# A two-layer encoder trunk on one core: later scores, scaled copies in the bias tiles, grouped head norms, two more warming products, token halves apart in the last unit

## The chip, the cores and the metric

The kernel runs on one core of a Trainium2 chip. The metric is device microseconds of one execution, as a median over several runs. Before the change it is 2175.67 us, the median of 3 runs that lie between 2174.48 and 2177.18 us. One further execution was taken by the hardware profiler; all rows below come from it.

## The reference, cut to what matters

256 tokens of width 2048 pass through two layers. Both have 16 heads of 128 and a squared-ReLU MLP of width 8192. Everything is float32.

```python
# layer 1
u = rms_norm(h, a_norm_g)
q, k, v, fz = split(u @ a_w_in)                 # 2048 -> 3*2048 + 16
q, k = rms_norm(q per head), rms_norm(k per head)
logf = log_sigmoid(fz + a_b_f)                  # c = cumsum over tokens
s = q @ k.T * scale + c[query] - c[key]         # causal
h = h + softmax(s) @ v @ a_w_out
h = h + sq(relu(rms_norm(h) @ w1)) @ w2
# shared keys and values
k, v = split(rms_norm(h) @ kv_w);  k = rms_norm(k per head)
# layer 2
q = rms_norm(rms_norm(h) @ b_w_q per head)
s = q @ k.T * scale + bias[clipped distance]    # by chunks of 64
h = h + softmax(s) @ v @ b_w_out
h = h + sq(relu(rms_norm(h) @ w1)) @ w2
```

## The kernel before, in words

**Weights and units.** Every weight matrix comes in *units* of 128 x 1024 float32 (512 KB): two slices of 128 rows of the inner dimension, for the same 512 output columns. A unit is loaded by SyncE (`load`, L128, tile `raw`, 4 buffers), split by ScalarE into a rounded part `hi` (L144) and by VectorE into the remainder `lo` (L145; `issue`, L137, 3 buffers each), and used by TensorE in 12 products of 512 columns (`products`, L318): for each of the 2 slices and each of the 2 blocks `b` of 128 tokens, activations-hi by weights-hi (L324), hi by lo (L325) and lo by hi (L326). `fetch` (L148) splits two units ahead of the one that is used and keeps three loads ahead of that. A *panel* (`panels`, L328) is 8 units: the whole inner dimension of 2048 for 512 output columns of both token blocks. Its sums stand in one of two PSUM tiles `acc` of two banks, one bank for each token block. After the last unit the panel's `evac` is called for block 0 and then for block 1. A *woven* stage runs its first two panels in turn, unit by unit.

**Order.** `keep_order` (L36) pins VectorE, ScalarE, TensorE and SyncE to the order in which the Python text issues their instructions. So each of the four is a queue in written order, and an instruction that waits holds back all that stand behind it on its engine. GpSimd has few instructions.

**The fill queue.** All work beside the products is put into `fill`, a list of lists. After the 12 products of each unit `run_fill` (L157) takes the next list and issues what is in it. `add_fill` (L457) lays a sequence of lists over the head of the queue, one list for each coming unit. So "item 7" of an added sequence is issued after the products of the eighth unit from then on. A unit takes about 2.7 us.

**Turning.** TensorE needs the inner dimension on the partitions. VectorE transposes blocks of 32 x 32 into a tile `z` (L210, 2 buffers); `carry` (L213) writes `z` to a DRAM tile `turn` with one transfer and, two units later (one for the small softmax tiles), reads it back with four transfers (L226), which SyncE can issue only when the first has landed.

**Layer 1 attention.** For each group of 4 heads there is a q panel, a k panel and a v panel. `head_norm` (L347) squares the sums on ScalarE (L356), adds them by head on VectorE (L358), forms the root on GpSimd (L364), and in later units scales and turns them (L368, L210). `attend` (L434) is added after the k panel: it makes the bias tile (items 2, 5, 6), and for head `a` of the group runs `softmax` in four steps from item 7 + 3a: the score products on TensorE (L396, L397), bias and maximum on VectorE, exponentials on ScalarE, division and transposition on VectorE. The turned probabilities `prT` come back over DRAM, and `values` (L425) uses them 8 items after the scores. In the last group of a layer the heads follow each other by 2 items.

**Between the layers.** `next_x` (L234) forms each new residual block, turns it, and `split_turned` (L185) scales it by the norm gains into a tile `y` of the `z` buffers (L190) and splits that into hi (L193) and lo (L194). At the end of layer 1 this is done twice, for layer 2's queries (`xb`) and, in reversed token order, for the shared keys and values (`xkv`, L626, items 13 to 20 of the query stage). The query stage has four panels, the first two woven. For its first group `head_norm` copies the sums out of PSUM first (`copied`, L354), so that the third panel can have the `acc` tile.

**Start and end.** Before the first weights are there, 9 products of ones run on TensorE (L89). At the end, L391 adds the last panel's sums to the residual for one token block after the other, and L673 stores each.

Of the kernel before, what the change touches and what calls it, by code (L numbers as in the profile page):

```python
# [9 lines left out]
F32 = mybir.dt.float32  # L10
F32R = mybir.dt.float32r
AF = mybir.ActivationFunctionType
ALU = mybir.AluOpType
AX = mybir.AxisListType

P = 128
T = 256
NB = T // P
D = 2048
KT = D // P  # L20
H = 16
GH = 4
NG = H // GH
# [6 lines left out]
EARLY = 3  # L30
UA = UN // 512
REL = 384
GAP = 3


def keep_order(tc, engines):  # L36
# [11 lines left out]
def trunk(ctx: ExitStack, tc: tile.TileContext, xT, xr, gs, hg, bf, wgate, w_in, w_oa, w1a, w2a,  # L48
          w_kv, w_qb, w_ob, w1b, w2b, rel, out):
    nc = tc.nc  # L50
    V, S, G, TE, SY = nc.vector, nc.scalar, nc.gpsimd, nc.tensor, nc.sync
# [8 lines left out]
    qkv = pool("qkv", 2)  # L60
# [24 lines left out]
    ones = const.tile([P, T], F32, name="ones")  # L85
    V.memset(ones, 1.0)
    warm = ps_o.tile([P, 512], F32, name="pt", tag="po")
    for _ in range(9):
        TE.matmul(warm[:, :P], ones[:, :P], ones[:, :P], start=True, stop=True)  # L89
    mhalf = const.tile([P, GH], F32, name="mhalf")  # L90
    V.memset(mhalf, -0.5)
# [92 lines left out]

    def split_turned(t, n, which, into):  # L185
        x = acts.tile([P, 2, GH, T], F32R, name="act")
        y = qkv.tile([P, GH * T], F32, name="z").rearrange("p (k t) -> p k t", k=GH)
        for j in range(GH):
            m = which * KT + GH * n + j
            S.activation(y[:, j].rearrange("p (b i c) -> p b i c", b=NB, i=4), t[:, j], AF.Copy, scale=gsb[:, m : m + 1])  # L190
            if j == 1:
                yield
        S.activation(x[:, 0], y, AF.Copy)  # L193
        V.tensor_tensor(x[:, 1], y, x[:, 0].bitcast(F32), op=ALU.subtract)  # L194
        into.extend(x[:, :, j, :] for j in range(GH))
        yield
# [16 lines left out]
    def carry(z, dst, wait=1):  # L213
        w = z.shape[1]
        n = w // 4
        box = []

        def rows():
            box.append(dram.tile([P, w], F32, name="turn", tag=f"turn{w}", bufs=4))
            SY.dma_start(box[0], z)  # L220

        def columns():
            s = box[0].rearrange("(i a) f -> a i f", i=4)
            d = dst.rearrange("p (i f) -> p i f", i=4)
            for j in range(4):
                SY.dma_start(d[32 * j : 32 * j + 32], s[:, :, j * n : (j + 1) * n])  # L226

        return [[rows]] + [[]] * wait + [[columns], [], []]
# [86 lines left out]
            f.r, f.e = root(f.ms, f.name), scaled(f.ms, f.name)  # L315
            self.flipped = f

    def products(ps, hi, lo, x, u):  # L318
        for j in range(UA):
            k = u * UA + j  # L320
            wh, wl = hi[:, j * 512 : (j + 1) * 512], lo[:, j * 512 : (j + 1) * 512]
            for b in range(NB):
                xh, xl = (x[k][:, i, b * P : (b + 1) * P] for i in range(2))
                TE.matmul(ps[b], xh, wh, start=k == 0, stop=False)  # L324
                TE.matmul(ps[b], xh, wl, start=False, stop=False)  # L325
                TE.matmul(ps[b], xl, wh, start=False, stop=k == KT - 1)  # L326

    def panels(x, evacs, before=None):  # L328
        ps = [acc_pair() for _ in evacs]
        for u in range(KT // UA):  # L330
            if before:
                before(u)
            for q, evac in enumerate(evacs):
                hi, lo = fetch(min(u // 2, AHEAD), 2) if before else fetch()
                products(ps[q], hi, lo, x, u)
                run_fill()
                if u == KT // UA - 1:
                    for b in range(NB):
                        evac(b, ps[q][b])
# [7 lines left out]
    def head_norm(stats, z, dst, late=0, copied=False):  # L347
        rest = []

        def f(b, ps):  # L350
            src = ps
            if copied:
                src = wk.tile([P, 512], F32, name="qc", tag="wk")
                V.tensor_copy(src, ps)  # L354
            sq = wk.tile([P, 512], F32, name="sq", tag="wk")
            S.activation(sq, ps, AF.Square)  # L356
            ss = sm.tile([P, GH], F32, name="ss")
            V.tensor_reduce(ss, sq.rearrange("p (a d) -> p a d", a=GH), axis=AX.X, op=ALU.add)  # L358
            rn = sm.tile([P, GH], F32, name="rn")

            def norm():
                vv = sm.tile([P, GH], F32, name="vv")
                V.tensor_scalar(vv, ss, 1.0 / P, stats().e[:, b : b + 1], op0=ALU.mult, op1=ALU.add)  # L363
                G.tensor_tensor(rn, vv, mhalf, op=ALU.pow)  # L364

            def turn():
                qn = wk.tile([P, 512], F32, name="qn", tag="wk")
                V.tensor_tensor(qn.rearrange("p (a d) -> p a d", a=GH), src.rearrange("p (a d) -> p a d", a=GH),  # L368
                                rn.unsqueeze(2).to_broadcast([P, GH, P]), op=ALU.mult)
                blocks32(qn, z, b)  # L370

            rest.append((norm, turn))
            if not late:
                norm()
            if b == NB - 1:
                add_fill([[]] * (late - 1) + ([[n for n, _ in rest]] if late else []) + [[t] for _, t in rest] + carry(z, dst))
        return f

    def scale_q(land, layer):
# [45 lines left out]
    def values(st, a, v, o, i):  # L425
        po = ps_o.tile([P, 512], F32, name="po", tag="po")
        pT = st["pT"].rearrange("p (i n c) -> p n i c", i=4, c=32)
        TE.matmul(po[:, :T], v[:, 0, a * P : (a + 1) * P], pT[:, :2], start=True, stop=False)  # L428
        TE.matmul(po[:, P:T], v[:, 1, a * P : (a + 1) * P], pT[:, 2], start=False, stop=True)  # L429
        o[i] = quarter(i)  # L430
        S.activation(o[i][:, 0], po[:, :T], AF.Copy)  # L431
        V.tensor_tensor(o[i][:, 1], po[:, :T], o[i][:, 0].bitcast(F32), op=ALU.subtract)  # L432

    def attend(g, q, k, v, cq, o, make_bias, gap):  # L434
        st = [{} for _ in range(GH)]
        box = {}
        k4 = k.rearrange("p (i a b c) -> p a b i c", i=4, a=GH, b=NB)
        items = [[] for _ in range(15 + gap * GH)]
        step = steps(lambda: make_bias(g, box))
        items[2].append(step)  # L440
        items[5].append(step)
        items[6].append(step)
        for a in range(GH):
            at = 7 + gap * a
            step = steps(lambda a=a: softmax(st[a], g, a, q(), k4, box["b"], cq() if cq else None))
            for i in range(4):
                items[at + i].append(step)
            items[at + 3].append(lambda a=a: add_fill(st[a]["carry"]))
            items[at + 8].append(lambda a=a: values(st[a], a, v, o, g * GH + a))
        return items  # L450

    def v_evac(v, r):
# [4 lines left out]
    def add_fill(items):  # L457
        for i, it in enumerate(items):
            if i < len(fill):
                fill[i] = fill[i] + it  # L460
            else:
                fill.append(it)
# [3 lines left out]
    x = []  # L466
# [33 lines left out]
    def gates(x, st):  # L500
# [44 lines left out]
        def turn_c():  # L545
            pc = ps_o.tile([P, 512], F32, name="pt", tag="po")
            ct["cq"] = const.tile([P, NB, H], F32, name="cq")
            for b in range(NB):
# [2 lines left out]

        step, spread = steps(logs), steps(st.spread)
        return [[clear], [], [parts], [lambda: products(range(8))], [lambda: products(range(8, KT))], [spread], [spread],
                [step], [step], [step], [], [], [turn_c]]

    def decay_bias(g, box):
        nb = qkv.tile([P, GH, REL], F32, name="bias")
# [11 lines left out]
    for g in range(NG):  # L569
        zq, lq = turned("z")  # L570
        qb = {}
        late = 6 if g == 0 else 0
        panels(x, [head_norm(lambda: st0, zq, lq, late)], begin if g == 0 else None)
        if g == 0:
            step = steps(head_gains)
            add_fill([[step], [], [], [], [step]])
            add_fill([[lambda i=i: rows_in(i)] for i in range(5, 8)])
            add_fill([[lambda i=i: st0.add(*chunks[i])] for i in range(3, 8)])
            fill[4].insert(len(fill[4]), st0.roots)
            add_fill(gates(x, st0))  # L580
        add_fill([[]] * (7 + late) + [[lambda qb=qb, lq=lq: qb.update(q=scale_q(lq, 0))]])
        zk, k = turned("k")
        v = qkv.tile([P, NB, 512], F32, name="v")
        panels(x, [head_norm(lambda: st0, zk, k)])
        add_fill(attend(g, lambda qb=qb: qb["q"], k, v, lambda: ct["cq"], o, decay_bias, GAP if g < NG - 1 else 2))
        panels(x, [v_evac(v, st0.r)])

    def mlp(x, st, last):
# [34 lines left out]
    mlp(x1, st1, lambda n, r2: next_x(n, r2, st2, 3, xb, kept))  # L623
    xkv = []
    again = [steps(lambda n=n: kept[n](True, 2, xkv)) for n in range(NG)]
    add_fill([[], [], [st2.both], [], [st2.flip]] + [[]] * 8 + [[again[i // 2]] for i in range(2 * NG)])  # L626


    qs, evs = [], []
# [26 lines left out]
    for g in range(NG):  # L656
        zk, k = turned("k")
        v = qkv.tile([P, NB, 512], F32, name="v")
        panels(xkv, [head_norm(lambda: st2.flipped, zk, k)])
        add_fill(attend(g, lambda g=g: qs[g], k, v, None, o, rel_bias, GAP if g < NG - 1 else 2))  # L660
        panels(xkv, [v_evac(v, st2.flipped.r)])

    st3, x3 = RowStats("n"), []
# [66 lines left out]
```

## Time and profile before

| | us |
|---|---|
| median of 3 runs | 2175.67 |
| the profiled execution | 2172.02 |
| its span in the trace | 2169.8 |
| TensorE busy in the span | 2151.4 (99%) |
| VectorE busy | 1280.5 (59%) |
| ScalarE busy | 1048.8 (48%) |

The page of the profile gives, for the whole span, busy time by engine and the costliest groups of instructions. The waits view adds up, for each engine and line, the time that the engine sat idle and what ended it. The timeline gives single instructions with start and duration; a product of 512 columns is shown as busy for 0.39 us, although in full flow the next starts 0.227 us after it, since successive products overlap in the array. So the time lost at a wait is the distance between two starts less 0.227 us, which is 0.16 us more than the idle time shown. The windows view gives the TensorE clock that was granted in a stretch, as a share of full speed.

### The profile page before, as it was taken

To read this page: it belongs to the slowest core of one execution; us is meant where nothing else is said; L and a number is where in the kernel's file an instruction comes from. 1 tells how busy PE (TensorE), PEld (TensorE's weight loads), DVE (VectorE), ACT (ScalarE), POOL (GpSimd) and SP (SyncE) were. 2 spreads that over 40 slices of the span, in tenths; PEclk is the share of its full clock that TensorE was granted. 3 is DMA by queue.
4 is the path that set the end of the run, shared out by engine and by line. 5 is a ranking of instruction groups with operands and counts; after the bars stand their busy time and mean duration, and the time that the engine had idled before them with its cause. 6 is when DMAs were issued, how large, how long until landed. Compare 5 with 4: busy or idle time off the path is not lost.

```text
span 2169.8 us, 25773 instructions
## 1 busy us (share of the span) xinstructions
PE 2151.4 (99%) x9514; PEld 1776.5 (82%) x9514; DVE 1280.5 (59%) x1465; ACT 1048.8 (48%) x1251; POOL 48.4 (2%) x47
## 2 busy tenths in 40 slices
PE   9999999999999999999999999999999999999999
PEld 8778888888888888888877888888888888888887
DVE  6767766655555555555667667765554555555554
ACT  6544445554344344345555445455543543443443
POOL 1010000000000000000001001000000000000000
PEclk9999999999999999999999999999999999999999
DMA  7776787786676577677767777777866766766774
GB/s 277 240 237 223 229 253 232 235 265 199 207 238 214 194 244 221 194 232 232 229 211 247 245 227 225 243 239 243 250 195 213 242 203 203 243 213 194 240 225 165
DMA packets 183886, 491.60 MB, mean 227 GB/s; under 512 B 36928, under 2 KB 73936, under 8 KB 183760
## 3 DMA queue, kind: packets, MB, share of 16 engines
q1 hardware_dynamic: 183760, 489.96, 71.7%
q8 instruction: 74, 1.21, 0.2%
q14 instruction: 52, 0.43, 0.1%
HBM read 450.01 MB, written 39.87 MB: 226 GB/s over the span
## 4 chain that ended last, share of the span: by engine, by line
PE 92%; DMA 4%; DVE 2%; ACT 1%; SPq 1%; issue 1%; DVEq 0%; ACTq 0%
PE acc L325 30%; PE acc L324 30%; PE acc L326 30%; DMA k<-turn 1%; DMA turn<-z 1%; DVE lo L145 1%; PE s L397 1%; PE po L428 1%; ACT hi L144 1%; SPq L226 0%; DMA prT<-turn 0%; PE s L396 0%; DMA raw<-in_w2a 0%; DVE qn L368 0%; PE po L429 0%
## 5 line engine op out<-in xcount | busy, mean ns | idle before, releaser
L145 DVE TENSOR_TENSOR lo<-raw,hi 128x1024 fp32r<-128x1024 f32 (+1 forms) x770 | 937.8, 1219 | 784.8 <-ACT hi L144 779.1
L144 ACT ACTIVATE hi<-raw 128x1024 fp32r<-128x1024 f32 (+1 forms) x770 | 812.6, 1057 | 1005.5 <-PE acc L326 931.0
L324 PE MATMUL acc<-hi,act 128*128 128x512 f32 x3072 | 1206.9, 393 | 2.7 <-ACT sq L356 2.3
L325 PE MATMUL acc<-lo,act 128*128 128x512 f32 x3072 | 1198.2, 390 | 3.5 <-DVE lo L145 3.4
L326 PE MATMUL acc<-hi,act 128*128 128x512 f32 x3072 | 1196.9, 390 | 0.0
L325 PEld LDWEIGHTS acc<-lo,act 128*128 128x128 f32 x3072 | 577.8, 188 | 126.6 <-DVE lo L145 8.4
L324 PEld LDWEIGHTS acc<-hi,act 128*128 128x128 f32 x3072 | 577.6, 188 | 122.4 <-ACT sq L356 2.7
L326 PEld LDWEIGHTS acc<-hi,act 128*128 128x128 f32 x3072 | 577.5, 188 | 120.6
L364 POOL TENSOR_TENSOR rn<-vv,mhalf 128x4 f32<-128x4 f32 x32 | 43.0, 1357 | 412.7 <-DVE vv L363 412.7
L210 DVE STREAM_TRANSPOSE z<-acc 128x512 f32<-128x512 f32 x64 | 42.0, 695 | 11.9 <-PE acc L326 11.9
L431 ACT ACTIVATE act<-po 128x256 fp32r<-128x256 f32 x32 | 12.3, 383 | 70.3 <-PE po L429 70.3
L600 DVE TENSOR_TENSOR act<-q,act 128x1024 fp32r<-128x1024 f32 x32 | 38.9, 1217 | 0.0
L597 ACT ACTIVATE act<-q 128x1024 fp32r<-128x1024 f32 x32 | 34.0, 1062 | 1.0
L593 ACT ACTIVATE q<-q 128x1024 f32<-128x1024 f32 x32 | 33.4, 1044 | 0.0
L599 ACT ACTIVATE q<-q 128x1024 f32<-128x1024 f32 x32 | 33.4, 1042 | 0.0
L432 DVE TENSOR_TENSOR act<-po,act 128x256 fp32r<-128x256 f32 x32 | 13.5, 423 | 31.5 <-ACT act L431 31.5
L358 DVE TENSOR_REDUCE ss<-sq 128x4 f32<-128x512 f32 x32 | 21.7, 681 | 16.5 <-ACT sq L356 16.5
L190 ACT ACTIVATE z<-q,gsb 128x256 f32<-128x256 f32 x64 | 28.6, 495 | 5.2 <-DMA turn<-z 5.1
L391 DVE SCALAR_TENSOR_TENSOR h<-acc,qn,h 128x512 f32<-128x512 f32 x32 | 22.6, 746 | 11.0 <-PE acc L326 11.0
L414 ACT ACTIVATE pr<-t,nm 128x128 f32<-128x128 f32 x64 | 28.3, 444 | 1.0 <-DVE nm L411 0.9
L391 DVE SCALAR_TENSOR_TENSOR h<-acc,qm,h 128x512 f32<-128x512 f32 x32 | 22.6, 747 | 5.5 <-PE acc L326 5.5
L194 DVE TENSOR_TENSOR act<-z,act 128x1024 fp32r<-128x1024 f32 x16 | 19.6, 1224 | 8.0 <-ACT act L193 8.0
(99 smaller groups left out, 426.8 us busy)
## 6 DMA issues: line engine op xcount, KB each, us to landing
raw<-in_w1a SPq DMA_DIRECT2D x128, 512.0 KB, 4.3
raw<-in_w2a SPq DMA_DIRECT2D x128, 512.0 KB, 3.9
raw<-in_w1b SPq DMA_DIRECT2D x128, 512.0 KB, 4.2
raw<-in_w2b SPq DMA_DIRECT2D x128, 512.0 KB, 4.2
raw<-in_w_in SPq DMA_DIRECT2D x94, 512.0 KB, 4.6
raw<-in_w_kv SPq DMA_DIRECT2D x64, 512.0 KB, 4.5
turn<-z SPq DMA_DIRECT2D x60, 512.0 KB, 3.9
q<-turn SPq DMA_DIRECT2D x176, 128.0 KB, 5.4
```

Source lines behind the costliest of these rows:

```text
L144: S.activation(hi[:, c], raw[:, c], AF.Copy)
L145: V.tensor_tensor(lo[:, c], raw[:, c], hi[:, c].bitcast(F32), op=ALU.subtract)
L210: V.transpose(z.rearrange("p (j n b c) -> p b n j c", j=4, n=n, b=nb)[:, b], src.rearrange("p (n j c) -> p n j c", n=n, j=4))
L324: TE.matmul(ps[b], xh, wh, start=k == 0, stop=False)
L325: TE.matmul(ps[b], xh, wl, start=False, stop=False)
L326: TE.matmul(ps[b], xl, wh, start=False, stop=k == KT - 1)
L364: G.tensor_tensor(rn, vv, mhalf, op=ALU.pow)
L391: V.scalar_tensor_tensor(hc, ps, r2[:, b : b + 1], hc, op0=ALU.mult, op1=ALU.add)
L593: S.activation(t, t, AF.Relu)
L597: S.activation(hi, t, AF.Square)
L599: S.activation(t, t, AF.Square)
L600: V.tensor_tensor(lo, t, hi.bitcast(F32), op=ALU.subtract)
```

## The change

It has six parts. (1) The scores of head `a` start at item 9 + 3a instead of 7 + 3a, and the values follow 9 items later instead of 8; in a layer's last group the scores start at items 8, 10, 12 and 13 instead of 7, 9, 11 and 13, the values 8 items later as before. The bias tile's three steps come one item later (3, 6, 7), and so do the three steps of the forget gate's logarithms (`logs`), whose sums the bias is loaded from. (2) `split_turned` takes its tile `y` from the `bias` buffers instead of the `z` buffers, and uses the first 256 of its 384 columns in each of the four rows. (3) In `head_norm` the additions by head (`total`) are issued for both token blocks after both squares, and where the sums are copied, the squares read the copy. (4) The forming of `xkv` starts at item 18 of the query stage instead of 13. (5) 11 warming products instead of 9. (6) In the very last unit of the kernel the 12 products are ordered by token block first.

```diff
-GAP = 3
...
-    for _ in range(9):
+    for _ in range(11):
         TE.matmul(warm[:, :P], ones[:, :P], ones[:, :P], start=True, stop=True)
...
     def split_turned(t, n, which, into):
         x = acts.tile([P, 2, GH, T], F32R, name="act")
-        y = qkv.tile([P, GH * T], F32, name="z").rearrange("p (k t) -> p k t", k=GH)
+        y = qkv.tile([P, GH, REL], F32, name="bias")[:, :, :T]
...
-    def products(ps, hi, lo, x, u):
-        for j in range(UA):
+    def products(ps, hi, lo, x, u, halves=False):
+        order = [(j, b) for j in range(UA) for b in range(NB)]
+        if halves:
+            order.sort(key=lambda i: i[1])
+        for j, b in order:
             k = u * UA + j
             wh, wl = hi[:, j * 512 : (j + 1) * 512], lo[:, j * 512 : (j + 1) * 512]
-            for b in range(NB):
-                xh, xl = (x[k][:, i, b * P : (b + 1) * P] for i in range(2))
...
+            xh, xl = (x[k][:, i, b * P : (b + 1) * P] for i in range(2))
...
-                products(ps[q], hi, lo, x, u)
+                products(ps[q], hi, lo, x, u, not units and not ready)
...
             sq = wk.tile([P, 512], F32, name="sq", tag="wk")
-            S.activation(sq, ps, AF.Square)
+            S.activation(sq, src, AF.Square)
             ss = sm.tile([P, GH], F32, name="ss")
-            V.tensor_reduce(ss, sq.rearrange("p (a d) -> p a d", a=GH), axis=AX.X, op=ALU.add)
             rn = sm.tile([P, GH], F32, name="rn")
+
+            def total():
+                V.tensor_reduce(ss, sq.rearrange("p (a d) -> p a d", a=GH), axis=AX.X, op=ALU.add)
...
-            rest.append((norm, turn))
-            if not late:
-                norm()
+            rest.append((total, norm, turn))
             if b == NB - 1:
-                add_fill([[]] * (late - 1) + ([[n for n, _ in rest]] if late else []) + [[t] for _, t in rest] + carry(z, dst))
+                for total, norm, _ in rest:
+                    total()
+                    if not late:
+                        norm()
+                add_fill([[]] * (late - 1) + ([[n for _, n, _ in rest]] if late else []) + [[t] for _, _, t in rest] + carry(z, dst))
...
-    def attend(g, q, k, v, cq, o, make_bias, gap):
+    def attend(g, q, k, v, cq, o, make_bias):
...
-        items = [[] for _ in range(15 + gap * GH)]
+        at, far = ((8, 10, 12, 13), 8) if g == NG - 1 else ((9, 12, 15, 18), 9)
+        items = [[] for _ in range(at[-1] + far + 1)]
         step = steps(lambda: make_bias(g, box))
-        items[2].append(step)
-        items[5].append(step)
-        items[6].append(step)
+        for i in (3, 6, 7):
+            items[i].append(step)
         for a in range(GH):
-            at = 7 + gap * a
...
             for i in range(4):
-                items[at + i].append(step)
-            items[at + 3].append(lambda a=a: add_fill(st[a]["carry"]))
-            items[at + 8].append(lambda a=a: values(st[a], a, v, o, g * GH + a))
+                items[at[a] + i].append(step)
+            items[at[a] + 3].append(lambda a=a: add_fill(st[a]["carry"]))
+            items[at[a] + far].append(lambda a=a: values(st[a], a, v, o, g * GH + a))
...
         return [[clear], [], [parts], [lambda: products(range(8))], [lambda: products(range(8, KT))], [spread], [spread],
-                [step], [step], [step], [], [], [turn_c]]
+                [], [step], [step], [step], [], [turn_c]]
...
-    add_fill([[], [], [st2.both], [], [st2.flip]] + [[]] * 8 + [[again[i // 2]] for i in range(2 * NG)])
+    add_fill([[], [], [st2.both], [], [st2.flip]] + [[]] * 13 + [[again[i // 2]] for i in range(2 * NG)])
```

## The prediction

> **What bounds the kernel now.** The page comes first: TensorE is busy for all but 18 us, so only its idle places can be won, unless the granted clock falls.
>
> ```profile
> PE 2151.4 (99%) x9514; PEld 1776.5 (82%) x9514; DVE 1280.5 (59%) x1465; ACT 1048.8 (48%) x1251; POOL 48.4 (2%) x47
> ```
>
> The waits view of TensorE says what those places are (sum, times, longest):
>
> ```profile
> PE s L396 <- DMA k<-turn: 4.7, 4, 2.0
> PE acc L325 <- DVE lo L145: 3.4, 4, 1.9
> PE acc L324 <- ACT sq L356: 2.3, 1, 2.3
> ...
> PE po L428 <- DMA prT<-turn: 0.9, 1, 0.9
> PE acc L324 <- ACT hi L144: 0.4, 1, 0.4
> PE s L396 <- issue: 0.3, 1, 0.3
> ```
>
> The reader is to see that scores wait for turned keys, values for turned probabilities, and ordinary products for the split of the weights and for a square that holds PSUM. The splitting engines run ahead: ScalarE waited for late loads in layer 1's attention, yet of ScalarE's lateness 0.4 us reached TensorE, at the very start.
>
> ```profile
> ACT hi L144 <- DMA raw<-in_w_in: 15.9, 11, 4.0
> ```
>
> The pitch of the products comes from the end of the timeline: three products in 0.68 us, so 0.227 us each, 2.73 us for a unit of 12. A product is shown as busy for 0.39 us, so each wait cost 0.16 us more than its idle time.
>
> ```profile
> 2163.76 0.39 PE L326 MATMUL acc<-hi,act 128*128 128x512 f32 x1
> ...
> 2164.44 0.39 PE L326 MATMUL acc<-hi,act 128*128 128x512 f32 x1
> 2164.87 1.41 DVE L391 SCALAR_TENSOR_TENSOR h<-acc,qn,h 128x512 f32<-128x512 f32 x2 [5.84 <-PE acc L326]
> ```
>
> **Scores and values later.** The five waits of the scores are 4.7 + 0.3 us idle and 5 x 0.16 us: 5.8 us. The longest is 2.0 + 0.16 = 2.2 us. Two units later is 5.5 us, in the last group one unit, 2.7 us; both cover it. What is late next would be the same keys if they landed over 3 us later (last group: over 0.5 us). The bias load now goes out one unit nearer to the keys' reads and shares the DMA engines with them; if that cover goes, it costs 1 to 2 us in the two last groups. Values get four units instead of three from score to use, but for the last groups: 0.9 + 0.16 = 1.1 us. Both gone: **6.9 us**. The number of products and turns does not change, and no instruction is added.
>
> The moved steps pass other work. On SyncE, the four reads of the third head's probabilities now stand behind the four reads of turned queries (layer 1) or keys (layer 2); before, the fourth head's write stood there, and its reads kept SyncE blocked from 197.15 to 203.72, since the write landed late:
>
> ```profile
> 196.30 0.38 SPq L220 DMA_DIRECT2D turn<-z  x1
> 196.77 0.38 SPq L134 DMA_DIRECT2D raw<-in_w_in  x1
> 203.72 1.74 SPq L226 DMA_DIRECT2D prT<-turn  x4
> ```
>
> A block of 6.6 us, with all weight loads behind it, starved TensorE of no weights. On VectorE, where the head sums are taken (item 15) and turned (16, 17), a division moves from 16 to 15 and 18, a bias addition from 17 to 16: the same pieces in another order. I bound new waits there and on SyncE by 0 and 3 us and take **0.5 us** against the change, near the lower end, for the loads that were up to 4.0 us late for ScalarE cost TensorE nothing. The forget gate's logarithms move one unit with their VectorE work; one of the four `lo` waits lies there, and the keys' turns now stand before part of it: 0, between -0.5 and +0.5 us.
>
> **The query stage.** Two edits meet here: grouped norms, and `xkv` five units later. TensorE's timeline:
>
> ```profile
> 1132.61 0.39 PE L326 MATMUL acc<-hi,act 128*128 128x512 f32 x1
> 1135.29 0.50 PE L324 MATMUL acc<-hi,act 128*128 128x512 f32 x1 [2.30 <-ACT sq L356]
> ...
> 1141.66 0.50 PE L325 MATMUL acc<-lo,act 128*128 128x512 f32 x1 [0.40 <-DVE lo L145]
> ...
> 1146.57 0.50 PE L325 MATMUL acc<-lo,act 128*128 128x512 f32 x1 [1.86 <-DVE lo L145]
> ```
>
> Idle plus 0.16 each: 2.46 + 0.56 + 2.02 = 5.0 us, and 0.1 us for the restart of each (0.34 between L325 and L326 there instead of 0.23): 5.4 us. VectorE shows why:
>
> ```profile
> 1130.58 1.23 DVE L194 TENSOR_TENSOR act<-z,act 128x1024 fp32r<-128x1024 f32 x1 [0.67 <-ACT act L193]
> 1131.72 0.68 DVE L354 COPY qc<-acc 128x512 f32<-128x512 f32 x1
> 1133.07 0.69 DVE L358 TENSOR_REDUCE ss<-sq 128x4 f32<-128x512 f32 x1 [0.66 <-ACT sq L356]
> 1133.79 0.23 DVE L363 TENSOR_SCALAR vv<-ss,eb 128x4 f32<-128x4 f32 x1
> 1133.92 0.69 DVE L354 COPY qc<-acc 128x512 f32<-128x512 f32 x1
> ...
> 1136.22 1.23 DVE L145 TENSOR_TENSOR lo<-raw,hi 128x1024 fp32r<-128x1024 f32 x1
> 1137.36 0.68 DVE L368 TENSOR_TENSOR qn<-qc,rn 128x512 f32<-128x512 f32 x1
> ...
> 1138.72 0.64 DVE L358 TENSOR_REDUCE ss<-sq 128x4 f32<-128x512 f32 x1
> 1139.39 0.23 DVE L363 TENSOR_SCALAR vv<-ss,eb 128x4 f32<-128x4 f32 x1
> 1139.53 0.68 DVE L358 TENSOR_REDUCE ss<-sq 128x4 f32<-128x512 f32 x1
> ...
> 1145.33 1.18 DVE L145 TENSOR_TENSOR lo<-raw,hi 128x1024 fp32r<-128x1024 f32 x1
> ```
>
> The copy that frees PSUM stands behind an `xkv` split (L194), the second copy behind the sum of the first square. From then on VectorE has no idle time and each `lo` is late. In the windows view that idle time also costs clock:
>
> ```profile
> 1133.50:1136.90 3.40, 1.61 (x7) 1.35 (x8) 2.66 (x6) 2.26 (x5) 1.54 (x2) 1.00 0.00 0
> ...
> 1143.72:1147.13 3.41, 1.55 (x7) 0.96 (x6) 3.36 (x5) 0.32 (x1) 0.00 (x0) 1.00 0.58 235
> 1147.13:1150.55 3.42, 3.42 (x10) 2.63 (x9) 1.94 (x2) 3.39 (x7) 0.00 (x0) 0.50 0.84 283
> ```
>
> After 1.55 us busy in 3.41 (first column after the length), the next 3.42 us ran at clock 0.50: another 1.7 us. In all 7.1 us.
>
> Now the new order, with steps from start to start of these rows: `lo` 1.14, a turn (scaling and transposition) 1.36, a sum with its small step 0.81, a copy 0.68. The first panel's sums are complete 2.73 us before the second's (1132.61 + 0.39), at 1130.27. Copies until 1131.7, 1.1 us before the third panel is due at 1132.84: that wait is gone. Squares end at 1132.3, so do two sums at 1133.3, ScalarE's next `hi` (1.06) at 1133.4. Then `lo` until 1134.5, a turn 1135.9, the second panel's two sums 1137.5, `lo` 1138.65 (due 1138.53), two turns 1141.4, `lo` 1142.5, due 1141.26 and by the first delay 1141.4. TensorE loses about 1.3 us, with restarts 1.4, and the idle share stays above that of the window that kept its clock (1.61 us busy). Gain 7.1 - 1.4 = **5.7 us**; bounds 1.5 (`lo` as late as now, one wait gone in part) and 7.1. `xkv` has its items 18 to 25 instead, under the third panel's products and before the kv panels at unit 32; the third panel's sums fall at 23, and a unit's slack covers one `L194` of 1.14. The `bias` tiles are idle in this stage, so L190's wait for `z` (5.1 us on ScalarE) goes; it lay inside the stall counted here. Reading rows of 256 out of 384 costs nothing that a row shows.
>
> **Warming.** The 9 products are 18 instructions:
>
> ```profile
> 1.18 4.21 PE L89 MATMUL pt<-ones 128*128 128x128 f32 x18 [1.18 <-DVE mhalf L91]
> ...
> 5.75 0.79 PE L324 MATMUL acc<-hi,act 128*128 128x512 f32 x1 [0.37 <-ACT hi L144]
> 6.48 0.79 PE L325 MATMUL acc<-lo,act 128*128 128x512 f32 x1
> ...
> 10.06 0.60 PE L324 MATMUL acc<-hi,act 128*128 128x512 f32 x1
> 10.48 0.41 PE L325 MATMUL acc<-lo,act 128*128 128x512 f32 x1
> ...
> 12.31 1.23 DVE L145 TENSOR_TENSOR lo<-raw,hi 128x1024 fp32r<-128x1024 f32 x1 [0.93 <-ACT hi L144]
> 13.93 0.39 PE L325 MATMUL acc<-lo,act 128*128 128x512 f32 x1
> ```
>
> Four more by 4.21 / 18 = 0.234 us end at 6.3, 0.6 us after the first real product could start, but L325 waits for its `lo` until 6.4 anyway: at most 0.3 us late. The gap at 5.4 to 5.75 is filled, and the clock, half until 10.48 (0.42 from start to start), may rise earlier. It cannot be used in full: the third unit's `lo`, after its load, ends at 13.54, and TensorE used it at 13.93. So **0.35 us** gained; bounds -0.3 and +1.7 (half of one 3.4 us window).
>
> The Trainium skill ("TensorE: Matmul & The Clock Gate", Part 1: The HAM clock gate) says that about 3.4 us of sustained work release the clock, in windows that run free of the kernel's start, and warns against fitting a count of cold products. The length of the dip above, 3.42 us, agrees. By the rule the clock would rise between 4.6 and 8.0 instead of 10.4, an estimate of 1.2 to 2.9 us; by the rows the data come too late for that.
>
> **The last unit by halves.** VectorE's first addition (2164.87) began after the last product, although its own block's last one started at 2163.76. In the changed kernel's instruction order it still waits for a count that only the kernel's last product raises, because both blocks are one PSUM tile. So **0**, where a true overlap would give 0.7.
>
> **Sum.** 6.9 - 0.5 + 5.7 + 0.35 = 12.4 us. The profiled execution took 2172.02 us, 2.2 more than its span; it would take 2159.6. It is 3.65 below the median of the runs, 2175.67; the same gain gives 2163.3.
>
> **Rivals.** (a) VectorE stays the bound in the query stage: for it speaks its unbroken work from 1130 to 1148, against it two splits of 1.14 less there and two copies together. Gain there 1.5 instead of 5.7: 2167.5. (b) The new order at items 15 to 18 delays `lo` in the six inner groups by one piece of 1.3 us: 7.8 us lost, 2171.1. For: that stretch is VectorE's densest in each group; against: it holds the same pieces. (c) Slower: SyncE's block. At unit 20 two sets of reads wait one after the other for their writes. `fetch` holds five units, 13.6 us, less a load's landing of 4 to 5 us and a split of 2.4: from a block of about 7 us on TensorE starves. With 11 us (6.6 and a second landing of 4) it is 4 us in six groups, each with a half-clock window of 1.7: 34 us, 2197. Against: the third head's write goes out a unit before those reads. (d) The halves overlap after all: 2162.6. (e) The clock rises by 7.0 us and the data keep pace: half of 3.5 us, 2161.9; for it the filled gap, against it the late `lo`.
>
> **How the numbers follow.** Forecast 0.60 (own range 2159 to 2167), (d) and (e), both inside it, 0.05 each, (a) 0.12, (b) 0.08, (c) 0.05; 0.05 for nothing named. Low end: 12.4 + 1.4 (no residue) + 1.35 (clock) + 0.7 + 0.5 = 16.4, so 2159; high end: (a) with 2.5 us of the bounded waits, 2170. A measurement tells 0.2%, 4.35 us, from no change: faster below 2171.3. The forecast, (d), (e), (a) and three quarters of (b) lie there: 0.88; same 0.07, slower 0.05.
>
> **What would show it.** Right: no wait of L396 for `k` and none of L428 outside the last groups; after the third panel's start one `lo` wait of about 1 us and no window at 0.50 behind it; the final additions still after the last product; the waits at 64 and 1078 us still there. Wrong: a wait of L324 on `hi` or `raw` in the attention panels, new `lo` waits 16 to 20 units into a group, or L396 still waiting in the last groups.

## The result and the profile after

The changed kernel takes 2163.64 us (median of 8 runs, 2159.19 to 2167.38) against 2175.45 us for the kernel before (8 runs, 2168.92 to 2181.84): a ratio of 0.9947, with a 95% interval of 0.9930 to 0.9965. A second set of runs gave 2161.96 against 2176.84 us, 0.9929 (0.9913 to 0.9945). The forecast was 2163.3 us.

The profiled execution took 2165.94 us with a span of 2163.2 us. Its lines are shifted by the edits: the products are L325, L326 and L327, the splits L143 and L144, the scores L401 and L402, the values L433 and L434. The page's first lines:

```profile
span 2163.2 us, 25790 instructions
...
PE 2148.5 (99%) x9518; PEld 1774.7 (82%) x9518; DVE 1279.1 (59%) x1465; ACT 1048.9 (48%) x1251; POOL 48.2 (2%) x47
```

The waits view of TensorE (sum, times, longest):

```profile
PE acc L326 <- DVE lo L144: 7.2, 13, 1.2
PE pt L88 <- DVE mhalf L90: 1.2, 1, 1.2
PE acc L327 <- DVE act L181: 0.5, 1, 0.5
PE acc L325 <- ACT act L180: 0.5, 1, 0.5
```

No score waits for keys any more, no value for probabilities, no product for a square. What is left is `lo` coming late, and there is more of it than before (7.2 us in 13 places, 3.4 us in 4).

Where the `lo` waits lie shows in the timeline. In the query stage, behind the second panel's end:

```profile
1137.58 0.39 PE L325 MATMUL acc<-hi,act 128*128 128x512 f32 x1
1138.16 0.50 PE L326 MATMUL acc<-lo,act 128*128 128x512 f32 x1 [0.19 <-DVE lo L144]
...
1140.80 0.39 PE L325 MATMUL acc<-hi,act 128*128 128x512 f32 x1
1141.93 0.50 PE L326 MATMUL acc<-lo,act 128*128 128x512 f32 x1 [0.74 <-DVE lo L144]
```

and VectorE beside it:

```profile
1129.62 1.29 DVE L355 COPY qc<-acc 128x512 f32<-128x512 f32 x2 [0.40 <-PE acc L327]
1131.01 0.69 DVE L362 TENSOR_REDUCE ss<-sq 128x4 f32<-128x512 f32 x1
...
1136.88 1.22 DVE L144 TENSOR_TENSOR lo<-raw,hi 128x1024 fp32r<-128x1024 f32 x1
...
1140.69 1.18 DVE L144 TENSOR_TENSOR lo<-raw,hi 128x1024 fp32r<-128x1024 f32 x1
```

The two copies now run together, as soon as the panel ends, so the third panel starts without a wait; 0.35 and 0.90 us are lost later, start to start less 0.227. In the windows view no stretch there is at half clock; the third window is the one that follows the second wait, as 1147.13 to 1150.55 did before (columns: length; busy time and count of TensorE, its weight loads, VectorE, ScalarE, GpSimd; granted clock; DMA share; GB/s):

```profile
1136.90:1140.30 3.40, 3.21 (x14) 2.36 (x13) 3.33 (x6) 1.86 (x3) 2.07 (x2) 1.00 0.32 84
1140.30:1143.70 3.40, 2.65 (x12) 1.83 (x12) 3.37 (x5) 2.67 (x4) 0.00 (x0) 1.00 0.74 251
1143.70:1147.10 3.40, 3.40 (x17) 2.79 (x16) 3.40 (x4) 2.11 (x4) 0.00 (x0) 1.00 0.96 306
```

At the start the clock is up early and the data are late:

```profile
7.05 0.39 PE L325 MATMUL acc<-hi,act 128*128 128x512 f32 x1
7.28 0.40 PE L326 MATMUL acc<-lo,act 128*128 128x512 f32 x1
...
12.82 0.49 PE L325 MATMUL acc<-hi,act 128*128 128x512 f32 x1
14.08 0.50 PE L326 MATMUL acc<-lo,act 128*128 128x512 f32 x1 [0.77 <-DVE lo L144]
```

Products are 0.23 us apart from 7.05 on; before, that came at 10.48. But the third unit's `lo` holds TensorE until 14.08 (13.93 before). And at the end both additions still follow the last product together:

```profile
2157.82 0.39 PE L327 MATMUL acc<-hi,act 128*128 128x512 f32 x1
2158.24 1.41 DVE L396 SCALAR_TENSOR_TENSOR h<-acc,qn,h 128x512 f32<-128x512 f32 x2 [5.84 <-PE acc L327]
```

### The profile page after: what moved, and what is told of

It reads as the page before. It is cut to its first block, busy times and chain, and to the rows that moved or that the text cites. A ratio compares the mean times of both kernels' runs of the same rounds, so it can differ in the third digit from the quotient of the medians.

```text
span 2163.2 us, 25790 instructions
## 1 busy us (share of the span) xinstructions
PE 2148.5 (99%) x9518; PEld 1774.7 (82%) x9518; DVE 1279.1 (59%) x1465; ACT 1048.9 (48%) x1251; POOL 48.2 (2%) x47
## 4 chain that ended last, share of the span: by engine, by line
PE 91%; DMA 5%; DVE 2%; ACT 1%; issue 1%; SPq 0%; DVEq 0%; ACTq 0%
PE acc L326 30%; PE acc L327 30%; PE acc L325 30%; DMA raw<-in_w_in 1%; DMA q<-turn 1%; DVE lo L144 1%; DMA turn<-z 1%; PE po L433 1%; PE s L402 1%; DMA z<-turn 1%; ACT hi L143 0%; DMA raw<-in_w2a 0%; DMA raw<-in_w_oa 0%; PE po L434 0%; PE s L401 0%
## 5 line engine op out<-in xcount | busy, mean ns | idle before, releaser
L144 DVE TENSOR_TENSOR lo<-raw,hi 128x1024 fp32r<-128x1024 f32 (+1 forms) x770 | 937.5, 1219 | 789.8 <-ACT hi L143 786.0
L143 ACT ACTIVATE hi<-raw 128x1024 fp32r<-128x1024 f32 (+1 forms) x770 | 813.1, 1057 | 990.3 <-PE acc L327 921.6
L325 PE MATMUL acc<-hi,act 128*128 128x512 f32 x3072 | 1204.6, 392 | 0.7 <-ACT act L180 0.5
L326 PE MATMUL acc<-lo,act 128*128 128x512 f32 x3072 | 1197.4, 390 | 7.2 <-DVE lo L144 7.2
L327 PE MATMUL acc<-hi,act 128*128 128x512 f32 x3072 | 1195.8, 389 | 0.5 <-DVE act L181 0.5
L326 PEld LDWEIGHTS acc<-lo,act 128*128 128x128 f32 x3072 | 576.8, 188 | 132.5 <-DVE lo L144 14.3
L325 PEld LDWEIGHTS acc<-hi,act 128*128 128x128 f32 x3072 | 576.8, 188 | 121.2 <-ACT hi L143 1.4
L327 PEld LDWEIGHTS acc<-hi,act 128*128 128x128 f32 x3072 | 576.6, 188 | 120.9 <-DVE act L181 1.0
L209 DVE STREAM_TRANSPOSE z<-acc 128x512 f32<-128x512 f32 x64 | 42.0, 695 | 11.8 <-PE acc L327 11.8
L189 ACT ACTIVATE bias<-q,gsb 128x256 f32<-128x256 f32 x64 | 28.6, 494 | 0.0
L357 ACT ACTIVATE sq<-acc 128x512 f32<-128x512 f32 x30 | 16.2, 593 | 16.0 <-PE acc L327 16.0
```

Source lines behind the costliest of these rows:

```text
L143: S.activation(hi[:, c], raw[:, c], AF.Copy)
L144: V.tensor_tensor(lo[:, c], raw[:, c], hi[:, c].bitcast(F32), op=ALU.subtract)
L209: V.transpose(z.rearrange("p (j n b c) -> p b n j c", j=4, n=n, b=nb)[:, b], src.rearrange("p (n j c) -> p n j c", n=n, j=4))
```

## The experiments

Each was timed against the kernel before on the same chip, and profiled once. Since single executions of one kernel differ by several us, the traces are compared by stage: the time between the first products of two units, counted over the whole kernel (767 is the last). Unit 16 begins the first group's v panel, and the query stage is 384 to 416. Layer 1's attention panels end at unit 96 and layer 2's at 480, but some of their scores and values are issued behind these marks, and more of them with the new items than with the old: between 416 and 480 TensorE runs 864 matmuls, the small ones of scores and values included, in the trace of before and 856 in that of after. So the stages are taken up to 112 and 496, where both have run the same number (1282 from unit 16 and 1088 from 416). Differences of 2 to 3 us lie within the intervals of the ratios; where a run's time cannot decide, the stage does.

```
profiled execution   start  16-112  384-400 400-416 416-496
                     to 8
before               30.05  292.07   46.25   48.17  240.99
again_before         31.29  290.34   46.25   48.18  243.06
scores_only          31.11  286.17   46.25   48.19  239.28
query_only           31.76  294.23   43.79   46.81  241.38
ends_only            30.75  291.20   46.25   48.15  240.31
after                31.96  286.66   43.79   46.27  239.28
again_after          31.56  284.36   43.79   47.71  239.28
no_ends              31.73  284.36   43.79   47.07  239.28
xkv_at_13            31.19  285.50   44.10   49.05  239.28
norms_apart          32.00  286.97   44.85   48.15  239.28
one_unit_later       31.42  284.35   43.79   48.23  239.28
two_tiles_end        31.54  285.80   43.79   46.43  239.28
xkv_in_two           31.23  284.79   43.79   46.77  239.28
both_mended          31.34  284.34   43.79   47.09  239.28
```

**The changed kernel again.** No edit.

> The changed kernel once more. Theory (chance): the waits behind late weight loads in its first profile (1.3 and 1.6 us before 28 us, 2 us at 84 to 90, 1.4 at 378, 1.3 at 1076) belong to that execution; in a second one those at the start and at 84 to 90 differ by over 1 us, while the lo waits of the query stage (0.4 and 0.9 us excess near 1138 and 1141, 0.4 and 0.5 near 1161 and 1167) come back within 0.1 us. Ratio to before 0.993 to 0.9965. Rival (order): all of them come back at the same places and sizes, since the new order of SyncE makes the loads late.

Ratio 0.9929 (0.9913 to 0.9945), span 2158.5 us. The waits at 84 to 90, 378 and 1076 us did not come back, those of the query stage near the second panel did, to 0.01 us (0.58 and 1.13 us from start to start both times). Those at the third panel's end came back longer: 0.83, 1.53 and 0.70 us from start to start near 1155 and 1162. At the start both theories were half right: the waits behind loads came again, within 0.5 us in all. So most late loads elsewhere differ from execution to execution, and the changed kernel's first profile, 4.7 us longer than its second, had many; at the start they belong to the kernel.

**The later scores alone.** On the kernel before:

```diff
-            at = 7 + gap * a
+        at, far = ((8, 10, 12, 13), 8) if g == NG - 1 else ((9, 12, 15, 18), 9)
...
-        items[2].append(step)
-        items[5].append(step)
-        items[6].append(step)
+        for i in (3, 6, 7):
+            items[i].append(step)
...
-                [step], [step], [step], [], [], [turn_c]]
+                [], [step], [step], [step], [], [turn_c]]
```

> The kernel before with the later scores, values, bias steps and logarithms alone. Theory: no wait of the score products for k and none of the value products for prT, 6.9 us less 0.5: ratio 0.997 (0.9955 to 0.9985); the three waits of the query stage stay with 5.4 us. Rival (SyncE or VectorE crowded): the score waits go, but the time falls by under 2 us, with new waits of acc products on lo or hi in the attention panels.

Ratio 0.9945 (0.9931 to 0.9960), 12 us (8.7 to 15.0) at 2176.84, more than expected. No wait for `k` or `prT` is left, the query stage stands as before (46.25 and 48.19 us).

**The query stage alone.** On the kernel before:

```diff
-        y = qkv.tile([P, GH * T], F32, name="z").rearrange("p (k t) -> p k t", k=GH)
+        y = qkv.tile([P, GH, REL], F32, name="bias")[:, :, :T]
...
-            S.activation(sq, ps, AF.Square)
+            S.activation(sq, src, AF.Square)
...
+                for total, norm, _ in rest:
+                    total()
+                    if not late:
+                        norm()
...
-    add_fill([[], [], [st2.both], [], [st2.flip]] + [[]] * 8 + [[again[i // 2]] for i in range(2 * NG)])
+    add_fill([[], [], [st2.both], [], [st2.flip]] + [[]] * 13 + [[again[i // 2]] for i in range(2 * NG)])
```

> The kernel before with the grouped norms, y in the bias tiles and xkv five units later alone. Theory: the query stage loses about 1.5 us at the second panel's norms and 1.1 at the third's instead of 5.4, and no window there is at clock 0.50: 4.5 to 6 us less, ratio 0.9976 (0.997 to 0.9985); the score waits stay with 5.8 us. Rival (VectorE stays the bound): the stage still loses 4 us or more, ratio above 0.999.

Ratio 0.9981 (0.9970 to 0.9992), 4.1 us at 2176.84. The stage fell from 94.4 to 90.6 us. This trace also shows that a long score wait costs more than its own length. One such wait, in the timeline, and the windows around it:

```profile
80.98 0.39 PE L326 MATMUL acc<-hi,act 128*128 128x512 f32 x1
85.15 0.77 PE L400 MATMUL s<-k,q 128*128 128x128 f32 x2 [3.78 <-DMA k<-turn]
85.71 1.06 PE L401 MATMUL s<-k,q 128*128 128x256 f32 x2
86.21 0.99 PE L324 MATMUL acc<-hi,act 128*128 128x512 f32 x1
```

```profile
78.00:84.43 6.43, 3.37 (x15) 2.44 (x14) 3.48 (x4) 3.11 (x4) 0.00 (x0) 1.00 1.08 233
84.43:91.25 6.82, 6.10 (x15) 4.90 (x16) 2.85 (x6) 1.21 (x2) 0.00 (x0) 0.50 0.82 307
```

The wait was 3.8 us in place of 2.0 at most in the prediction's trace, and the stretch of 6.82 us behind it ran at half clock: with TensorE busy for 6.10 us of it, about 3 us more were lost.

**The two ends alone.** 11 warming products and the order by halves on the kernel before.

> The kernel before with 11 warming products and the last unit by token halves alone. Theory: the clock rises one window (3.4 us) earlier in this profile or not, worth 0.35 us (at most 1.7); the first final addition still starts after the last product: ratio 0.9992 to 1.0002. Rival (halves overlap): the first final addition starts 0.7 us before the last product's end, and the time falls by 1 us or more.

Ratio 0.9988 (0.9977 to 0.9999), 2.6 us: the rival's size, though the interval reaches into the theory's range. The rival's mechanism is not in the trace, which has no gain at the end: from the start of the last product to the end of the span pass 5.4 us, as in the trace of before (2169.8 - 2164.44).

**The changed kernel without its ends.** `range(11)` back to `range(9)`, and no `halves`.

> The changed kernel with 9 warming products and the last unit in the old order again. Theory: the ends are worth nothing, since loads bound the start (unit 8 begins at 30.0 to 32.0 us whether the clock rose at 4.8 or at 10.5) and 5.38 us pass from the last product to the end in every trace so far: ratio to before as for the changed kernel's own second timing, 0.9929, within 0.0010. Rival (the ends carry the 0.9988 of their own run): ratio 0.9941 or more.

Ratio 0.9942 (0.9928 to 0.9955), which is the rival's number; but its interval overlaps that of again_after, and the times themselves are alike: 2162.11 us, against 2162.27 for one_unit_later, which has both ends and was timed in the same set of runs, and 2161.96 for again_after in another set. Its trace has the same span as that of again_after, 2158.5 us. In it the clock rose late, between these two products:

```profile
10.06 0.42 PE L325 MATMUL acc<-hi,act 128*128 128x512 f32 x1
10.32 0.39 PE L326 MATMUL acc<-lo,act 128*128 128x512 f32 x1
```

and yet unit 8 began at 31.73 us. Over all traces the clock record begins at full speed between 4.0 and 7.0 us in the nine with 11 products, at 4.8, 5.9, 10.1, 10.1 and 10.5 us in the five with 9. Unit 8 begins at 30.75 to 32.00 us with 11 and at 30.05 to 31.76 with 9. So with two more products the clock rose by 7.0 us every time, with 9 in two traces of five, and the start does not get shorter. The two ratios that speak for a gain of 2 to 3 us by the ends are not explained by any trace; such a gain is neither shown nor excluded.

**xkv early again.** In the changed kernel:

```diff
-    add_fill([[], [], [st2.both], [], [st2.flip]] + [[]] * 13 + [[again[i // 2]] for i in range(2 * NG)])
+    add_fill([[], [], [st2.both], [], [st2.flip]] + [[]] * 8 + [[again[i // 2]] for i in range(2 * NG)])
```

> The changed kernel with xkv at items 13 to 20 again. Theory (VectorE's queue): the split stands ahead of the copies again, which end 1.1 us later: the third panel starts 0 to 0.5 us late, and the two lo waits behind it grow by 1.1 us each split, from 1.5 us in all to 3 to 4; units 400 to 416 lose 1.1 us less in exchange: 43.8 us for units 384 to 400 stays or grows by 0.5, units 400 to 416 take 48.0 to 49.5 instead of 46.3 to 47.7. Rival (the grouped norms do it all): units 384 to 416 take 90.0 to 91.5 us as in the changed kernel.

2162.78 us, ratio 0.9941 (0.9928 to 0.9953). The stage takes 93.15 us, as the first theory said: the third panel sits idle 0.2 us for a square, and the second `lo` wait is 2.29 us from start to start instead of 1.13. It brought the half clock back:

```profile
1137.30:1140.68 3.38, 1.50 (x6) 1.24 (x7) 3.33 (x5) 2.27 (x4) 0.00 (x0) 1.00 0.57 170
1140.68:1144.10 3.42, 3.42 (x9) 2.67 (x8) 3.18 (x3) 1.04 (x2) 0.00 (x0) 0.50 0.92 308
```

**The head norms apart again.** The old `head_norm` in the changed kernel.

> The changed kernel with the old head norms (each block's square and sum before the next block's copy, squares from PSUM). Theory: the first copy can start at once, but the second stands behind the first square and sum and PSUM is free only after the second square: the third panel starts 1.0 to 1.4 us late, behind a square; the lo waits behind it stay about 1.5 us in all; units 384 to 416 take 91 to 92.5 us. No window at clock 0.50. Rival (the moved xkv does it all): no wait for a square, 90.0 us.

2164.45 us, ratio 0.9949 (0.9936 to 0.9961). The third panel waits for a square:

```profile
1128.96 0.39 PE L327 MATMUL acc<-hi,act 128*128 128x512 f32 x1
1130.25 0.50 PE L325 MATMUL acc<-hi,act 128*128 128x512 f32 x1 [0.90 <-ACT sq L357]
```

1.06 us late, as expected; the stage took 93.0 us, 0.5 over the range, since the waits near the third panel's end were long this time. So undoing the grouped norms costs about 1.1 us where the panel starts (44.85 against 43.79 for units 384 to 400).

**One unit later instead of two.** In the changed kernel:

```diff
-        at, far = ((8, 10, 12, 13), 8) if g == NG - 1 else ((9, 12, 15, 18), 9)
+        at, far = ((8, 10, 12, 13), 8) if g == NG - 1 else ((8, 11, 14, 17), 9)
```

> The changed kernel with the scores at items 8, 11, 14, 17 in all but the last groups, so one unit later than before instead of two. Theory (the waits vary with the transfers: longest 2.2, 3.9 and 3.2 us in the three traces with the old items): one unit, 2.7 us, covers most but not all of them: waits of L401 for k of 0 to 1.5 us in all, time within 2 us of the changed kernel's. Rival (the new places in the panels are what counts, not the landing): the time goes halfway back, ratio 0.996 or more, with lo waits in the attention panels.

2162.27 us, ratio 0.9939 (0.9926 to 0.9951): the changed kernel's time. No wait for `k` was left in its trace.

**The last panel in two PSUM tiles.** In the changed kernel:

```diff
         ps = [acc_pair() for _ in evacs]
+        if len(units) + len(raws) + len(ready) == KT // UA:
+            ps[0][1] = ps_s.tile([P, 512], F32, name="s")
```

> The changed kernel whose last panel has its second token block's sums in another PSUM tile (the one of the scores), so that the first block's addition waits for its own six products alone. Theory (one tile held the additions together): 4.7 us from the start of the last product to the end instead of 5.38, so 0.6 to 0.7 us in the profile; too little for the ratio, 0.9922 to 0.9942 as for the changed kernel. Rival (the end of the last transfer decides): still 5.38 us.

Now the first addition runs beside the second block's products:

```profile
2152.69 0.39 PE L327 MATMUL acc<-hi,act 128*128 128x512 f32 x1
...
2153.12 0.75 DVE L398 SCALAR_TENSOR_TENSOR h<-acc,qn,h 128x512 f32<-128x512 f32 x1 [4.48 <-PE acc L327]
...
2154.05 0.39 PE L327 MATMUL s<-hi,act 128*128 128x512 f32 x1
2154.48 0.75 DVE L398 SCALAR_TENSOR_TENSOR h<-s,qn,h 128x512 f32<-128x512 f32 x1 [0.61 <-PE s L327]
```

4.55 us from the last product's start to the end of the span (2158.6), 0.83 less than with one tile; the first block's store is out of the way as well. 2159.81 us, ratio 0.9924 (0.9909 to 0.9939).

**xkv in two parts.** In the changed kernel, items 18 to 21 and 26 to 29:

```diff
-... + [[]] * 13 + [[again[i // 2]] for i in range(2 * NG)])
+... + [[]] * 13 + [[again[i // 2]] for i in range(4)] + [[]] * 4 + [[again[i // 2]] for i in range(4, 8)])
```

> The changed kernel with the last two quarters of xkv at items 26 to 29 instead of 22 to 25, behind the third panel's head norms. Theory (the lo waits near unit 408 come from the split standing ahead of the third panel's sums and turns): units 400 to 416 take 46.0 us or less in place of 46.3 to 48.2, the two waits there go and none comes before unit 416; time 1 us less than the changed kernel's, not to be told in the ratio. Rival (late loads make them): the waits stay within 0.3 us.

2162.99 us, ratio 0.9936 (0.9922 to 0.9950), the stage in 90.56 us: no gain, and the theory fell for the larger of the two waits. With no `xkv` split near, the wait at the third panel's end, in unit 410, stayed (0.50 and 1.53 us from start to start). The smaller one in unit 412, 0.66 to 0.70 us from start to start in all seven traces with `xkv` at items 18 to 25, is gone, here and in both_mended; so about 0.5 us did belong to the `xkv` split. ScalarE's timeline in that trace:

```profile
1149.71 1.15 ACT L386 ACTIVATE q<-z,gqk 128x1024 f32<-128x1024 f32 x1 [1.58 <-DMA z<-turn]
1151.60 1.06 ACT L143 ACTIVATE hi<-raw 128x1024 fp32r<-128x1024 f32 x1 [0.74 <-PE acc L326]
1154.23 1.15 ACT L386 ACTIVATE q<-z,gqk 128x1024 f32<-128x1024 f32 x1 [1.57 <-DMA z<-turn]
1155.28 1.06 ACT L357 ACTIVATE sq<-acc 128x512 f32<-128x512 f32 x2
1156.24 1.06 ACT L143 ACTIVATE hi<-raw 128x1024 fp32r<-128x1024 f32 x1
```

ScalarE twice waits for the turned queries of the first two panels (L386, scaling them, 7 units after each panel), and behind it stand the third panel's squares and the next `hi`. In the traces of the changed kernel the wait at this place has a late load and an L386 just ahead of the squares. Whether a later L386 frees it was not tried.

**Both.** The last two edits together.

> Both of the former edits on the changed kernel. Theory: 0.65 + 1.3 us together: ratio to before 0.9925, under the changed kernel's of the same chip by 0.0009, inside the interval; in the profile 4.7 us at the end and units 384 to 416 in 90.0 us or less. Rival: the SyncE transfers of the moved quarters meet the kv panel and cost what was won.

2159.05 us, ratio 0.9920 (0.9906 to 0.9934), the lowest of all, though its interval holds the ratios of two_tiles_end and again_after; 4.57 us at the end (2158.6 - 2154.03), the stage in 90.9 us, not under 90.0. What the traces show of a gain is the two tiles' alone.

**The kernel before once more.** No edit.

> The kernel before once more, for its waits. Theory (its first profiled execution, 2172.0 us against a median of 2175.5 to 2176.8, had few of them): the waits of the scores for k are longer this time, 5 to 10 us in all, or bring a window at clock 0.50 in the attention panels; the three waits of the query stage come back within 0.2 us, with the 0.50 window behind them. Rival (the profiled waits are typical, and the later scores win something else): 4.5 to 5.5 us again, no window at 0.50 outside the query stage.

2174.03 us. The waits view:

```profile
PE acc L325 <- DVE lo L145: 4.4, 6, 1.9
PE po L428 <- DMA prT<-turn: 3.1, 4, 1.4
PE s L396 <- ACT v L454: 2.3, 1, 2.3
PE acc L324 <- ACT sq L356: 2.3, 1, 2.3
...
PE s L396 <- DMA k<-turn: 1.0, 2, 0.6
```

Neither theory in full: the scores waited 3.3 us, less than the first time, of which the view puts the longest down to ScalarE's evacuation of v (L454), and the values 3.1 us instead of 0.9. No half clock outside the query stage. Each half of the query stage came back to 0.01 us, with its half-clock window.

## Why the prediction was right, and where its terms were off

**The sum.** 12.4 us was forecast; the two sets of runs gave 11.8 and 14.9. By stages it is made of other parts than forecast: 8.7 us instead of 6.4 from the scores and values, 3.5 instead of 5.7 from the query stage, nothing shown from the warming. The first two errors, 2.3 and 2.2 us, nearly cancel. The mechanisms were largely right, but that the sum fits this well is luck.

**Scores and values, 6.9 less 0.5 us.** The mechanism is shown: scores_only moves these steps alone, its trace has none of the waits, and it gives 12 us (8.7 to 15.0). In the traces, units 16 to 112 and 416 to 496 together take 531.5 to 535.6 us with the old items (mean of four 533.4) and 523.6 to 526.3 with the new ones (mean of nine 524.7; one_unit_later 523.6): 8.7 us less, at the low end of what the runs give; where the rest of the 12 us lies is open. The waits themselves were priced well. Single ones vary with the transfers: in unit 23 they were 1.6, 2.3, 3.8 and 3.0 us idle in the four traces. But all waits of scores and values add up to 5.9, 6.4, 6.0 and 5.0 us idle, and the 5.9 of the prediction's trace is near the middle. What the term left out is two other things. First, the one wait of 3.8 us cost a half-clock stretch as well, about 3 us more in one trace of four. Second, the new items let the fourth head's scores and the first head's values fall into one unit (item 18), three times in each layer. From the changed kernel's timeline:

```profile
186.00 0.39 PE L327 MATMUL acc<-hi,act 128*128 128x512 f32 x1
186.22 0.59 PE L433 MATMUL po<-prT,v 128*128 128x256 f32 x2
186.65 0.38 PE L434 MATMUL po<-prT,v 128*128 128x128 f32 x2
186.87 0.39 PE L401 MATMUL s<-k,q 128*128 128x128 f32 x2
187.10 0.60 PE L402 MATMUL s<-k,q 128*128 128x256 f32 x2
187.34 0.58 PE L325 MATMUL acc<-hi,act 128*128 128x512 f32 x1
187.76 0.40 PE L326 MATMUL acc<-lo,act 128*128 128x512 f32 x1
```

From the last product before (186.00) to the second after (187.76) pass 1.76 us. Alone, the same stretch takes 1.12 us for values (195.51 to 196.63) and 1.12 for scores (181.84 to 182.96 in the kernel before); together less one regular step of 0.23 that is 2.01. So 0.25 us is saved, 1.5 us over six places, which the prediction did not see. The cover of two units held, and one would have been enough in the trace of one_unit_later. The allowance of 0.5 us for new waits was about right in layer 1: there ordinary products sat idle for 0.5 to 2.2 us behind `lo` and `hi` in the nine traces with the full new items (mean 1.1) and for 0.4 to 0.5 us with the old ones. It was not needed in layer 2, where units 416 to 496 took 239.28 us in all nine. Rivals (b) and (c) did not happen.

**The query stage, 5.7 us.** The working was right as far as it went: the third panel starts on time, the residue behind the second panel was worked out as 1.3 us and measured 0.35 + 0.90 = 1.25, and the half-clock window is gone. The stage gained 3.5 us on average (94.4 against 90.1, 91.5, 90.9, 90.6, 92.0 and 90.2 us in after, again_after, no_ends, query_only, one_unit_later and two_tiles_end). The step that failed is "a unit's slack covers one `L194`" at the third panel's sums, which put the loss there at nothing: a new loss of 0.9 to 2.7 us stands there in each of those traces. xkv_in_two shows that only about 0.5 us of it is L194's; the cause of the rest, in unit 410, stays open, and the late load and L386 ahead of the squares are the candidates that the traces show. That both edits are needed is shown: without the one or the other the stage takes 93 us. The tile `y` in the `bias` buffers was not undone alone, so its share is not known. One reading was too strong: VectorE's work was not unbroken from 1130 us on; it waited 0.66 us for a square twice, ahead of 1133.07 and of 1135.27, and was without a gap only from there to 1147.86.

**Warming, 0.35 us.** The reason given for the small size, late data, agrees with the traces: the clock was up by 7.0 us in all nine with 11 products, and the start was no shorter. That the loads set its pace was not tried. By the rule of the Trainium skill ("TensorE: Matmul & The Clock Gate", Part 1: The HAM clock gate) the prediction put the rise between 4.6 and 8.0 us. Eight of the nine traces agree with that (5.05 to 7.04). In xkv_at_13 it came at 4.04 us, 2.9 us after the first warming product, so after less than the 3.4 us of sustained work that the Trainium skill states.

**The halves, 0.** Shown by both sides: 5.4 us at the end with one tile in either order, 4.55 with two. The 0.7 us named for a true overlap measured 0.83.

**Own signs.** As stated, the `lo` waits at 69 us (0.85 from start to start) and near 1076 us are still there, but the latter came and went from trace to trace. New `lo` waits in an attention panel did occur in the profile after (84 to 90 us, units 25 and 26), though not at the place that the prediction had named as a sign of error, 16 to 20 units into a group. They are not in the second profile, but they are not that execution's alone either: six of the nine traces with the scores two units later have waits in these two units, 0.1 to 1.7 us idle, and none of the other five has. In the profile after, ScalarE waited there 5.38 and 2.48 us for loads; whether the old order hides such late loads behind its score wait in unit 23 was not tried.

## What to carry to other kernels

A single wait read off one trace is one draw: where it hangs on a transfer, look at several executions, and add the half clock that a long one can bring. Before two kernels are compared by stage, make sure that both do the same work between the marks: moved work that falls behind a mark looks like a gain. When work is moved in a queue in written order, count everything that will stand ahead of the next urgent instruction at the new place, the waits of its neighbours too. And before an instruction order is changed to let two things overlap, look at what the waiting instruction really counts: halves of one tile were one thing.

## What the runs showed of the hardware

In the query stage the granted clock fell for one window of 3.4 us in five traces, each time after 3.41 us with 1.49 to 1.55 us of busy time on TensorE (ends_only 1.49, again_before and xkv_at_13 1.51, scores_only 1.53, before 1.55). It did not fall after 1.61 us in 3.40 (before, 1133.50) or 1.70 in 3.41 (ends_only, 81.61). That a window need not be idle for the clock to fall was not expected: here it fell at 46% busy and less and stayed at 47% and more. And a late start of the clock showed no cost here: with full speed only from 10.1 to 10.5 us, unit 8 began at 30.05, 31.29 and 31.73 us, with full speed by 7.0 us at 30.75 to 32.00. What sets the loads' pace at the start was not tried.
